# Layer A's masked score products as 32x32 diagonal blocks in one kept PSUM tile, and the norms' column sums from 32 stationary columns at a time

## The chip, the cores and the metric

The kernel runs on one core of one Trainium2 chip. The metric is the device time of one execution in microseconds (us): the median of 3 runs. The profile is of one further execution, taken with the hardware profiler, and its span is the time from its first to its last instruction. TensorE is called PE in the profile, VectorE DVE, ScalarE ACT, GpSimd POOL, and SyncE, which issues the DMAs, SP.

## What is computed

One inference step of a two-layer decoder trunk for 1024 prompt tokens and 8 single-token samples, all in fp32. Layer A is a gated linear recurrence (HGRN2) with 8 heads of 128 key and 256 value channels, layer B a spatial gating unit. Each layer starts with an RMS norm over the 1024 channels, and each is followed by a gated per-layer input with a norm of its own; a fifth norm ends the trunk. Cut to what matters here:

```python
def rmsnorm(x, g):
    return x * rsqrt(mean(x * x, axis=-1) + EPS) * g

def step(S, inp):                         # per chunk; b = cumsum of the log forget gates
    o_inter = einsum('bthk,bhkv->bthv', qb * exp(b), S)
    diff = where(causal, b[:, :, None] - b[:, None, :], -inf)
    att = einsum('bthk,bshk,btshk->btsh', qb, kb, exp(diff))
    o = o_inter + einsum('btsh,bshv->bthv', att, vb)
    S = exp(b_last) * S + einsum('bshk,bshv->bhkv', kb * exp(b_last - b), vb)
```

`att` is a masked score matrix whose decay between the two tokens depends on the channel. The kernel forms it for blocks of 128 tokens.

## The kernel before

**Tokens.** The 1032 tokens lie along the free axis, channels on the 128 partitions, in three chunks `c` of 384, 384 and 264 tokens (`W`); the first 256 of the last chunk are prompt tokens. `NT = (3, 3, 2)` counts the 128-token blocks of a chunk.

**Order of the work.** PE's instructions are issued in the order in which the program writes them (`manual_schedule`). The program writes the large projections (`proj`, L309, three fp32r products per 128x128 weight tile in `mm3`, L229 to L231) one after another, and between them runs small generator processes by a counter, `Ticks`: a projection of one chunk counts one tick at its half and, with its caller, one at its end, and a process that yields `n` goes on `n` ticks later. The instructions of the other engines are ordered by a planner by their place in the program and a priority (`tc.high_priority`). SP issues the DMAs in its queue's order.

**Layer A.** For each head `h` the projections f, q, the values (two halves) and the gate z (two halves) run over the three chunks. Beside them each chunk has a process `decay` (L661), which makes the score matrix in three parts, by the distance of the two tokens in a block of 128:

- Tokens of one group of 8: `X` and `Y` are q and k with decay factors about the middle of their group of 8 (L678 to L681). Four ticks later PE forms `Y^T X` for each block of 128 tokens into the PSUM tile `p0` (L685, one fp32 matmul of 128 stationary and 128 moving columns per block), and DVE copies the entries that `mask[:, 0]` names, 8x8 blocks on and above the diagonal, into the SBUF tile `am` (L696).
- Tokens of one group of 16 but of different groups of 8: DVE scales q and k in place, level by level (L722, L723, levels 1, 2, 4, ...). At level 8 PE forms `k^T q` in the same way into `p8` (L701), and DVE copies what `mask[:, 1]` names (L709).
- Larger distances: at levels 16, 32 and 64 PE forms only the rectangles that are wanted, 16x16, 32x32 and 64x64, into the tile `pC` (L719), which is kept for all of layer A and zeroed once (L563). DVE adds `am` and `pC` (L728).

`p0` and `p8` are both taken from one PSUM buffer (tag `pA`, one buffer), so each waits until DVE has read the one before. An fp32 matmul shows as two records in the trace, an fp32r matmul as one.

Other small PE work of layer A that the text names: transposes of the values (`pt_v`, L645), of k (`pt_k`, L738) and of the output (`pt_o`, L765), the state and output products (`pd`, `po`), and the samples' product `pos` (L856), in which eight fp32 matmuls of 32 stationary and 256 moving columns go in turn to PSUM partitions 0, 32, 64 and 96.

From head 1 on, the program order at chunk `c` is such that `pC` of one chunk (L719) is followed at once by `Y^T X` of the next chunk (L685).

**The norms.** `norm_sum` (L266) forms the sum of squares of each token over the partitions: for each block of 128 tokens and each part of the squares a matmul with the 128x128 squares stationary and one column of ones moving, into one column of the PSUM tile `pss` (L279). The first norm has four parts, the other four norms one (two in the last chunk). Then DVE adds epsilon (`rms_e`, L282), POOL takes the power -1/2 (`rsq`, L238), PE spreads the result over the partitions (`pbc`, L290) and DVE scales the rows (L303). Five norms of three chunks make 15 calls. In the first norm the calls stand between the per-layer input products (`ps_pple`) and the first projections.

## Time and profile before

| | before |
|---|---|
| median of 3 runs (lowest to highest) | 1895.23 us (1894.97 to 1897.35) |
| span of the profiled execution | 1892.0 us |
| mean granted TensorE clock | 0.994 |
| instructions of PE, DVE, ACT, POOL | 13130, 2977, 1859, 409 |
| records of the products L685 and L701 | 128 and 128 |
| records of the norms' sums L279 | 168 |

The profiled execution ran 1892.0 us from its first to its last instruction; the median of the runs is 3.2 us above that. A timeline row gives the start in us, the duration, the engine, the line and what is written and read, with `x6` for six records merged into one row. PE's matmuls overlap in it: the duration of one is its way through the array, and what it costs the next is the interval between their starts. `128*32 128x256` means 128 rows by 32 stationary columns, and an output of 256 columns. A row of the windows gives a stretch, its length, then for each engine that worked the busy time and the number of instructions in it, then the granted clock, the DMA share and GB/s.

### The profile page before, as it was taken

How to read it: one execution, taken by the hardware profiler on the slowest of the kernel's cores; microseconds unless marked ns; L12 is line 12 of the kernel's file. 1: busy time of each engine (PE TensorE's matmuls, PEld its weight loads, DVE VectorE, ACT ScalarE, POOL GpSimd, SP SyncE). 2: the span in 40 equal slices, each digit the busy share in tenths (PEclk: the TensorE clock that was granted, in tenths of full speed). 3: DMA queues.
4: the chain of work that ended last, by engine and by line, in shares of the span. 5: the costliest groups of instructions: out<-in, count | busy, mean ns of one | idle time of the engine just before them, and what ended most of it. 6: DMA issues, size and time to landing. Idle time of an engine off the chain costs nothing.

```text
span 1892.0 us, 34411 instructions
## 1 busy us (share of the span) xinstructions
PE 1861.4 (98%) x13130; PEld 1831.9 (97%) x13130; DVE 1331.5 (70%) x2977; ACT 866.1 (46%) x1859; POOL 396.2 (21%) x409
## 2 busy tenths in 40 slices
PE   9999999999999999999999999999999999999997
PEld 8999999999999999999999999999999999999997
DVE  5967677767767687678665845577777878777644
ACT  6463545444544546435344544433344335444342
POOL 4110001010000100000133333345544442000222
PEclk8999999999999999999999999999999999999998
DMA  6232323332222345854233343323334546953223
GB/s 216 75 108 78 109 73 111 126 130 97 94 79 93 101 139 158 287 194 135 94 127 119 115 143 92 95 79 116 111 116 148 184 134 205 302 184 106 63 90 113
DMA packets 155478, 243.15 MB, mean 129 GB/s; under 512 B 15088, under 2 KB 130480, under 8 KB 154288
## 3 DMA queue, kind: packets, MB, share of 16 engines
q1 hardware_dynamic: 155312, 240.94, 39.2%
q8 instruction: 103, 1.69, 0.4%
q14 instruction: 63, 0.52, 0.1%
HBM read 175.49 MB, written 65.40 MB: 127 GB/s over the span
## 4 chain that ended last, share of the span: by engine, by line
PE 81%; DVE 10%; DMA 5%; ACT 2%; issue 2%; POOL 1%; SPq 0%; DVEq 0%; ACTq 0%; POOLq 0%
PE ps_proj L229 19%; PE ps_proj L231 19%; PE ps_proj L230 19%; PE ps_o L229 2%; PE ps_o L230 2%; PE ps_o L231 2%; PE ps_d L229 2%; PE ps_d L231 2%; PE ps_d L230 2%; PE pC L719 1%; PE psp L1457 1%; DVE wlo L152 1%; PE pt_o L765 1%; PE p L685 1%; PE pt_v L645 1%
## 5 line engine op out<-in xcount | busy, mean ns | idle before, releaser
L229 PE MATMUL ps_proj<-bh,whi 128*128 128x384 f32 (+1 forms) x2392 | 764.9, 320 | 2.3 <-ACT pple_t L348 1.6
L231 PE MATMUL ps_proj<-bh,wlo 128*128 128x384 f32 (+1 forms) x2392 | 749.3, 313 | 1.5 <-DVE wlo L152 1.4
L230 PE MATMUL ps_proj<-bl,whi 128*128 128x384 f32 (+1 forms) x2392 | 748.0, 313 | 1.5 <-POOL bl L225 1.5
L229 PEld LDWEIGHTS ps_proj<-bh,whi 128*128 128x128 f32 x2392 | 451.0, 189 | 4.4 <-ACT pple_t L348 1.7
L230 PEld LDWEIGHTS ps_proj<-bl,whi 128*128 128x128 f32 x2392 | 451.4, 189 | 2.5 <-POOL bl L225 2.5
L231 PEld LDWEIGHTS ps_proj<-bh,wlo 128*128 128x128 f32 x2392 | 449.9, 188 | 2.7 <-DVE wlo L152 2.7
L152 DVE TENSOR_TENSOR wlo<-wstg,whi 128x1024 fp32r<-128x1024 f32 x148 | 184.6, 1248 | 97.7 <-ACT whi L151 96.3
L151 ACT CAST whi<-wstg 128x1024 fp32r<-128x1024 f32 x148 | 155.0, 1047 | 145.0 <-PE ps_proj L230 127.8
L151 ACT CAST shi<-ssum 128x512 fp32r<-128x512 f32 x128 | 79.1, 621 | 153.1 <-PE ps_proj L230 81.3
L152 DVE TENSOR_TENSOR slo<-ssum,shi 128x512 fp32r<-128x512 f32 x128 | 96.6, 757 | 8.5 <-ACT shi L151 8.0
L238 POOL TENSOR_TENSOR rsq<-rms_e,mhalf 128x3 f32<-128x3 f32 x15 | 14.1, 940 | 368.3 <-DVE rms_e L282 368.3
L229 PE MATMUL ps_proj<-xmh,shi 128*128 128x384 f32 x244 | 83.0, 340 | 1.1 <-DVE u L978 1.1
L231 PE MATMUL ps_proj<-xmh,slo 128*128 128x384 f32 x244 | 81.7, 335 | 0.0
L230 PE MATMUL ps_proj<-xml,shi 128*128 128x384 f32 x244 | 81.6, 335 | 0.0
L225 POOL TENSOR_TENSOR ql<-q,qh 128x384 fp32r<-128x384 f32 (+1 forms) x24 | 22.3, 929 | 254.0 <-ACT qh L224 254.0
L722 DVE TENSOR_TENSOR q<-q,t 128x192 f32<-128x192 f32 (+1 forms) x144 | 47.5, 331 | 39.1 <-PE pC L719 32.7
L229 PE MATMUL ps_o<-bh,whi 128*128 128x384 f32 (+1 forms) x232 | 73.2, 315 | 0.0
L230 PE MATMUL ps_o<-bl,whi 128*128 128x384 f32 (+1 forms) x232 | 72.7, 313 | 0.0
L231 PE MATMUL ps_o<-bh,wlo 128*128 128x384 f32 (+1 forms) x232 | 72.7, 313 | 0.0
L1466 POOL TENSOR_TENSOR s<-s,u 128x384 f32<-128x384 f32 (+1 forms) x48 | 54.7, 1140 | 68.5 <-DVE s L1460 67.9
L1205 DVE TENSOR_TENSOR tmp<-tmp,pj 128x384 f32<-128x384 f32 (+1 forms) x48 | 25.4, 530 | 56.4 <-ACT tmp L1204 50.4
L238 POOL TENSOR_TENSOR rsq<-ss_e,mhalf 128x3 f32<-128x3 f32 (+2 forms) x32 | 24.1, 752 | 192.9 <-DVE ss_e L759 192.9
(347 smaller groups left out, 3966.8 us busy)
## 6 DMA issues: line engine op xcount, KB each, us to landing
wstg<-in_wina SPq DMA_DIRECT2D x48, 512.0 KB, 3.7
wstg<-in_winb SPq DMA_DIRECT2D x48, 512.0 KB, 3.5
pj<-ppd SPq DMA_DIRECT2D x16, 516.0 KB, 5.0
S<-in_st SPq DMA_DIRECT2D x16, 512.0 KB, 4.6
vb<-vd SPq DMA_DIRECT2D x16, 512.0 KB, 4.8
out_so_s<-S SPq DMA_DIRECT2D x16, 512.0 KB, 3.5
wstg<-in_wouta SPq DMA_DIRECT2D x16, 512.0 KB, 3.5
wstg<-in_wgate SPq DMA_DIRECT2D x16, 512.0 KB, 3.7
```

Of the source, the lines that this page charges most:

```text
L151: A.copy(hi, src)
L152: V.tensor_tensor(lo, src, hi.bitcast(F32), ALU.subtract)
L225: last["lo"] = eng.tensor_tensor(lo, src, hi.bitcast(F32), ALU.subtract)
L229: PE.matmul(ps, wh, xh, start=first, stop=False, skip_group_check=more)
L230: PE.matmul(ps, wh, xl, start=False, stop=False, skip_group_check=more)
L231: PE.matmul(ps, wl, xh, start=False, stop=last, skip_group_check=more)
L238: G.tensor_tensor(y, e, mhalf[:, :n], ALU.pow)
L645: PE.transpose(pt[:, i, :], vf[:, i * P:(i + 1) * P], ident)
L685: PE.matmul(blk(p0, i), blk(Y, i), blk(X, i), start=True, stop=True)
L722: V.tensor_tensor(ql[:, :, 1, :], ql[:, :, 1, :], t2[:, :, 0:1].broadcast_to([P, n, lv]), ALU.mult)
L1205: V.tensor_tensor(gt[:, :w], gt[:, :w], pj[:, OFF[c]:OFF[c] + w], ALU.mult)
L1466: G.tensor_tensor(s[:, :w], s[:, :w], us[mm, c][:, :w], ALU.mult)
```

## The change

The two products are formed as 32x32 blocks on the diagonal alone, into one PSUM tile `pD` that is kept through layer A and zeroed once like `pC`; it takes the place of `p0` and `p8` in the tag `pA`. What lies outside the 32x32 blocks stays zero and is never copied, since both masks name entries within groups of 16. A product of a 128-token block is four matmuls of 32 stationary and 32 moving columns, each with all 128 rows, whose outputs lie at PSUM partitions 0, 32, 64 and 96. In `norm_sum` each matmul is likewise cut into four with 32 stationary columns, with outputs at the same four partition offsets.

```diff
@@ norm_sum
             for j, t in enumerate(parts):
-                PE.matmul(pss[:, i:i + 1], t[:, o:o + P], ones[:, 0:1],
-                          start=j == 0, stop=j == len(parts) - 1)
+                for b in range(0, P, 32):
+                    PE.matmul(pss[b:b + 32, i:i + 1], t[:, o + b:o + b + 32], ones[:, 0:1],
+                              start=j == 0, stop=j == len(parts) - 1)
@@ before layer A
     V.memset(pC, 0.0)
+    pD = pp.tile([P, 384], F32, name="pD", tag="pA", bufs=1)
+    V.memset(pD, 0.0)
@@ new
+    def diag(c, kt, qt):
+        for o in range(0, NT[c] * P, 32):
+            b = o % P
+            PE.matmul(pD[b:b + 32, o:o + 32], kt[:, o:o + 32], qt[:, o:o + 32], start=True, stop=True)
@@ decay
         yield 4
-        p0 = pp.tile([P, 384], F32, name="p0", tag="pA", bufs=1)
-        for i in range(NT[c]):
-            PE.matmul(blk(p0, i), blk(Y, i), blk(X, i), start=True, stop=True)
+        diag(c, Y, X)
...
-                V.copy_predicated(am[:, :w], mask[:, 0, :w], p0[:, :w])
+                V.copy_predicated(am[:, :w], mask[:, 0, :w], pD[:, :w])
...
-                p8 = pp.tile([P, 384], F32, name="p8", tag="pA", bufs=1)
-                for i in range(NT[c]):
-                    PE.matmul(blk(p8, i), blk(k, i), blk(q, i), start=True, stop=True)
+                diag(c, k, q)
...
-                V.copy_predicated(am[:, :w], mask[:, 1, :w], p8[:, :w])
+                V.copy_predicated(am[:, :w], mask[:, 1, :w], pD[:, :w])
```

## The prediction

> **What bounds the kernel now.** I read the page first, then the waits of the two engines that share layer A, then the timeline around each step that changes. The page's first part and its chain:

> ```profile
> PE 1861.4 (98%) x13130; PEld 1831.9 (97%) x13130; DVE 1331.5 (70%) x2977; ACT 866.1 (46%) x1859; POOL 396.2 (21%) x409
> ...
> PE 81%; DVE 10%; DMA 5%; ACT 2%; issue 2%; POOL 1%; SPq 0%; DVEq 0%; ACTq 0%; POOLq 0%
> ```

> The busy share of PE alone would prove little, since matmul ends are modelled; the chain says the same, that what ended last was 81% PE work. The waits between 60 and 760 us, where layer A runs (us in total, times, longest):

> ```profile
> PE pt_o L765 <- DVE oz L814: 5.0, 8, 1.6
> PE pt_v L645 <- DVE vl L225: 0.5, 1, 0.5
> PE pt_v L645 <- ACT vf L595: 0.2, 1, 0.2
> ...
> DVE Am L696 <- PE p L685: 23.9, 8, 4.4
> ```

> The first three lines are all of PE's waits there, 5.7 us in 700. None is for operands of the products (L685, L701). DVE, the next busiest engine, waits for PE and not the other way round. So an interval taken from PE in layer A should shorten the layer, and prices are to be read as intervals between matmul starts, not as durations.

> **Today's price of the two products.** Each is issued per 128-token block as one fp32 matmul with 128 stationary columns, which the trace records as two records:

> The timeline (start, duration, engine, line, records merged into the row) shows such a burst, and further on the sample product L856, which is needed below:

> ```profile
> 81.52 0.34 PE L231 MATMUL ps_proj<-bh,wlo 128*128 128x384 f32 x1
> 81.70 0.83 PE L685 MATMUL p<-X,Y 128*128 128x128 f32 x6
> 82.28 0.37 PE L229 MATMUL ps_proj<-bh,whi 128*128 128x264 f32 x1
> 82.49 0.28 PE L230 MATMUL ps_proj<-bl,whi 128*128 128x264 f32 x1
> ...
> 118.79 0.28 PE L230 MATMUL ps_proj<-bl,whi 128*128 128x264 f32 x1
> 118.91 0.28 PE L231 MATMUL ps_proj<-bh,wlo 128*128 128x264 f32 x1
> 119.13 1.07 PE L856 MATMUL pos<-S,qm 128*32 128x256 f32 x16
> 120.13 0.44 PE L229 MATMUL ps_proj<-bh,whi 128*128 128x384 f32 x1
> 120.41 0.34 PE L230 MATMUL ps_proj<-bl,whi 128*128 128x384 f32 x1
> 120.58 0.34 PE L231 MATMUL ps_proj<-bh,wlo 128*128 128x384 f32 x1
> ```

> ```profile
> L685 PE MATMUL p<-X,Y 128*128 128x128 f32 x128 | 19.6, 286 | 0.0
> ```

> From 81.52 to 82.49 are 0.97 us. Two ordinary intervals would be 0.17 (120.41 to 120.58, 384 columns) and 0.12 (118.79 to 118.91, 264 columns), so six records cost 0.68 us, 0.113 each, with nothing extra for going in or out. The group's row counts 128 records for L685, and by the code L701 has as many: 24 bursts each, 16 of six (chunks 0 and 1) and 8 of four (chunk 2).

> **The new price.** After the change the same bursts have four times as many records of 32 stationary by 32 moving columns, rotating over PSUM partitions 0, 32, 64, 96. The trace of before has this form already: L856 (32 stationary and 256 moving columns, the same rotation) and part of pC. Going into L856, 118.91 to 119.13 is 0.22 against 0.12: 0.10 us extra. Coming out, the second interval, 120.13 to 120.41, is 0.28 against 0.17: 0.105 extra. How many records had begun by a given moment is in the windows (the count behind PE busy), first L856, then pC:

> ```profile
> 119.05:119.16 0.11, 0.03 (x4) 0.04 (x5) 0.00 (x0) 1.00 0.00 0
> 119.05:119.36 0.31, 0.23 (x4) 0.16 (x8) 0.00 (x0) 1.00 0.00 0
> 119.05:119.40 0.35, 0.27 (x8) 0.19 (x12) 0.00 (x0) 1.00 0.00 0
> 119.05:119.84 0.79, 0.71 (x16) 0.42 (x16) 0.00 (x0) 1.00 0.00 0
> ...
> 97.60:97.83 0.23, 0.17 (x25) 0.17 (x26) 0.00 (x0) 1.00 1.11 387
> 97.60:98.01 0.41, 0.35 (x36) 0.35 (x36) 0.00 (x0) 1.00 1.11 377
> ```

> Four records start within 0.03 us, then none for 0.2 us, then the next four: four blocks in four column groups stream side by side, and a batch takes about 0.215 us for 256 moving columns (16 records in four batches, 1.00 us from 119.13 to 120.13, of which 0.025 is the first weights and 0.1 the drain at the end). In pC 25 records of (nearly all) 16 columns start in 0.17 us, under 7 ns each; the next 11, of 32 columns in only two groups, take 0.18, so 15 to 16 ns each, that is 0.03 us for one record in every group. With four groups I therefore take 0.03 us for a batch of four records, 7.5 ns each. The bounds are 6.5 (the spacing in pC and of four starts in L856) and 15 ns (no gain from four groups over two).

> A burst of B batches then costs: 0.10 in, 0.025 first weights, 0.03(B-1) for the starts, 0.02 inside the last batch, 0.125 from its last start to the next matmul (0.03 stream, 0.1 drain), 0.105 after: 0.345 + 0.03B. Six batches: 0.525 against 0.68, four: 0.465 against 0.45. A lone burst of chunk 0 or 1 gains 0.155, one of chunk 2 loses 0.015. The neighbours matter:

> ```profile
> 167.95 1.02 PE L719 MATMUL pC<-q,k 128*16 128x16 f32 x42
> 168.91 0.94 PE L685 MATMUL p<-X,Y 128*128 128x128 f32 x6
> 169.68 0.49 PE L645 MATMUL pt_v<-ident,vf 128*128 128x128 f32 x3
> 169.92 0.42 PE L229 MATMUL ps_proj<-bh,whi 128*128 128x384 f32 x1
> ...
> 84.86 0.55 PE L645 MATMUL pt_v<-ident,vf 128*128 128x128 f32 x3
> 85.17 0.37 PE L229 MATMUL ps_proj<-bh,whi 128*128 128x264 f32 x1
> ```

> - Transposes behind a burst take 0.24 us after full-width products (169.68 to 169.92) and 0.31 after pC (84.86 to 85.17): coming out costs them 0.07, not 0.105, so a burst of six there saves 0.68 - 0.10 - 0.32 - 0.07 = 0.19. These are L685 of chunk 0 (8) and L701 of chunk 0 and, from head 1, chunk 1 (15): 23 x 0.19 = 4.4.
> - From head 1 on, L685 of chunks 1 and 2 stands right behind pC of the chunk before, which pays for coming out today (168.91 to 169.68 is 0.77). There six records go from 0.77 to 0.32 + 0.07: 0.38 saved, 7 times, 2.7; four go from 0.54 to 0.26 + 0.105: 0.18, 7 times, 1.3.
> - Two lone bursts of head 0: 0.3. Nine of chunk 2: 0.1 lost.

> Layer A: 4.4 + 2.7 + 1.3 + 0.3 - 0.1 = 8.6 us. What DVE does with the products (L696, L709) keeps its size. pD's wait for DVE's last read is the wait that the tag's one buffer had; it was not among PE's waits. The added memset of pD on DVE is like pC's, 0.38 us:

> ```profile
> L563 DVE MEMSET pC<- x1: 378/378/378, 55.0 to 55.0; 128x384 f32 x1
> ```

> DVE's waiting for PE hides it; uncovered, 0.4. Layer-A ticks are counted in projections, so no wait of PE gets nearer by more than a fraction of a us.

> **The norms.** Their stationary side is the 128-column load, their moving side one column:

> ```profile
> L279 PE MATMUL pss<-ones,ssq 128*128 128x1 f32 x72 | 9.8, 237 | 0.0
> L279 PE MATMUL pss<-ones,sq 128*128 128x1 f32 x72 | 8.2, 246 | 0.0
> L279 PE MATMUL pss<-ones,sql 128*128 128x1 f32 x24 | 4.4, 251 | 1.4 <-ACT sql L258 1.4
> ...
> 14.33 2.73 PE L279 MATMUL pss<-ones,sq 128*128 128x1 f32 x24
> 16.92 0.42 PE L229 MATMUL ps_pple<-ph,whi 128*128 128x384 f32 x1
> ```

> 24 records take 2.59 us, 0.108 each, near the 0.113 above, which I use (2.7 for 24). The 168 records are three bursts of 24 (first norm), eight of 6 and four of 12 (the other four norms; two parts in the last chunk). By the same formula: six, 0.68 to 0.525, eight times 0.155 = 1.2; twelve, 1.36 to 0.705, three times 0.655 = 2.0. The fourth burst of twelve is in the tail, where only ACT's last squares are waited for:

> ```profile
> 1879.53 0.38 PE L279 MATMUL pss<-ones,sql 128*128 128x1 f32 x2 [1.40 <-ACT sql L258]
> ```

> Behind that wait stand ten records, 1.1 us, and become forty, about 0.35: 0.7 off the end of the program, since everything after it waits for this sum. For the first norm 24 batches give 1.065; no row shows 96 such records in a row, so I take 1.2 and save 1.5 per burst, 4.5 in all, if the start follows PE. At the second burst it does:

> ```profile
> 27.01 0.16 DVE L282 TENSOR_SCALAR rms_e<-pss 128x3 f32<-128x3 f32 x1 [1.75 <-PE pss L279]
> ...
> 27.74 0.51 ACT L224 CAST bh<-tmp 128x384 fp32r<-128x384 f32 x1 [1.92 <-DVE tmp L303]
> ...
> 28.59 0.69 PE L229 MATMUL ps_proj<-bh,whi 128*128 128x384 f32 x1 [1.61 <-ACT pple_t L348]
> ...
> 17.62:21.10 3.48, 3.48 (x14) 3.48 (x13) 0.00 (x0) 1.77 (x4) 2.54 (x3) 0.51 1.04 343
> ```

> DVE stands in its queue at rms_e until the burst is over, ACT behind DVE, and PE behind ACT. The last row (clock, third number from the end) says that the clock was halved right after the first long burst; a shorter burst may avert that, worth up to 1.7 us, which I leave to the range. So is the other end: another load or POOL's sums hold the start, and only one burst's 1.5 counts.

> **Sum.** 8.6 + 1.2 + 2.0 + 0.7 + 4.5 = 17.0 us off the profiled 1892.0, so a span of 1875.0; the median of the runs lies 3.2 above the span, which gives 1895.2 - 17.0 = 1878.2.

> [...] In L856 four records start within 0.03 us, in pC 25 within 0.17. [...]

> **Rivals.**
> - *Records in a long burst are bound by issue (slower).* The change adds 768 records to the products and 504 to the norms, 1696 in all now, so each ns per record is 1.7 us. At 7.5 ns 17.0 are saved, so break-even lies at 7.5 + 17.0/1.7 = 17.5 ns. If queued records run out and each then costs 22.5 ns, three times as much, 15 x 1.7 = 25.5 us are lost: 8.5 slower, 1903.7. For it: 96 records in a row were never seen. Against it: pC starts 36 in 0.35 us. Chance 0.06. [...]
> - *Two groups at a time, not four*: 15 ns per record, 7.5 x 1.7 = 12.7 less saved, 1890.9. Against it: L856's batches of four. Chance 0.08.
> - *PE's gain turns into waits* (a planner order that moves because PE has more instructions, DVE or the weights' loads late): about 1893 to 1895. For it: pt_o already waits for DVE. Against it: DVE waits more for PE than PE for DVE. Chance 0.06.

> **Numbers.** Main case 0.80, 1878.2. Its own ends: 6.5 ns per record (1.7 less) and the clock kept (1.7 and some of the start's chain) down to 1873; one burst alone of the start (+3.0), 10 ns per record (+4.2), up to 1885, to 1887 with some planner loss. So 1873 to 1887, which leaves out the rivals. A measurement of this kernel tells 0.2% (3.8 us) from nothing: faster (under 1891.4) 0.80 + 0.08, same 0.06, slower 0.06.

> **What would show it.** The products at 24 records in about 0.2 us from first start to last, lone bursts about 0.16 shorter between the surrounding projections, those behind pC 0.4; heads 1 to 6 each about 1.1 us shorter (0.38 + 0.18 + three times 0.19); long norm bursts of 1.0 to 1.3 us; the first projection (28.59) 1.5 to 4 us earlier; no new wait of PE on DVE. Wrong if records start 15 ns or more apart, if coming out costs more than 0.23 us, or if PE's idle time grows by what its bursts lose.

## The result and the profile after

The changed kernel takes 1878.1 us (median of 4 runs, 1875.5 to 1879.8), the kernel before beside it 1895.1 (1894.1 to 1897.4): a ratio of 0.9912, with an interval of 0.9898 to 0.9926. A second set of runs gave 1876.1 (ratio 0.9899, 0.9883 to 0.9915). The profiled spans are 1892.0 before and 1878.0 after. Lines move by one to four: L279 is now L280, L685 and L701 are both L663, pC's L719 is L723, the transposes' L645 is L648.

The page's first part and its chain, of after:

```profile
PE 1844.7 (98%) x14402; PEld 1802.6 (96%) x14402; DVE 1332.6 (71%) x2978; ACT 866.0 (46%) x1859; POOL 400.9 (21%) x409
...
PE 83%; DVE 8%; DMA 4%; ACT 2%; issue 1%; POOL 1%; SPq 0%; DVEq 0%; ACTq 0%; POOLq 0%
```

PE has 1272 records more and is busy 16.7 us less; the chain is still PE's. The groups of PE's shapes show the new records, four times as many with 32 stationary columns:

```profile
L663 PE MATMUL pD<-X,Y 128*32 128x32 f32 x512 | 9.0, 200 | 0.0
...
L280 PE MATMUL pss<-ones,ssq 128*32 128x1 f32 x288 | 5.1, 174 | 0.0
```

PE's busy time on the first product fell from 19.6 us (128 records) to 9.0 (512). The timeline of after, at the places that the prediction used:

```profile
14.65 0.98 PE L280 MATMUL pss<-ones,sq 128*32 128x1 f32 x96
15.56 0.44 PE L229 MATMUL ps_pple<-ph,whi 128*128 128x384 f32 x1
...
22.38 0.44 PE L229 MATMUL ps_proj<-bh,whi 128*128 128x384 f32 x1
...
74.75 0.34 PE L231 MATMUL ps_proj<-bh,wlo 128*128 128x384 f32 x1
75.02 0.40 PE L663 MATMUL pD<-X,Y 128*32 128x32 f32 x24
75.35 0.39 PE L229 MATMUL ps_proj<-bh,whi 128*128 128x264 f32 x1
75.57 0.29 PE L230 MATMUL ps_proj<-bl,whi 128*128 128x264 f32 x1
...
160.76 1.02 PE L723 MATMUL pC<-q,k 128*16 128x16 f32 x42
161.72 0.40 PE L663 MATMUL pD<-X,Y 128*32 128x32 f32 x24
162.04 0.55 PE L648 MATMUL pt_v<-ident,vf 128*128 128x128 f32 x3
162.35 0.42 PE L229 MATMUL ps_proj<-bh,whi 128*128 128x384 f32 x1
...
248.91 1.02 PE L723 MATMUL pC<-q,k 128*16 128x16 f32 x42
```

- The lone burst: 74.75 to 75.57 is 0.82 us, against 0.97 before. Going in costs 0.27 (0.17 without), coming out 0.33 to the next matmul and then 0.22 instead of 0.12.
- Behind pC: 160.76 to 162.35 is 1.59, against 1.97 before (167.95 to 169.92): 0.38 less.
- From one head's pC to the next, 160.76 to 248.91, are 88.15 us; before, the row `257.22 ... pC` follows the one at 167.95 after 89.27. So a head is 1.12 us shorter.
- The first norm's burst lies 0.91 before the next matmul, against 2.59, and 96 records of it start in 0.82 us:

```profile
14.64:14.85 0.21, 0.20 (x23) 0.20 (x27) 1.00 1.05 380
14.64:15.05 0.41, 0.40 (x47) 0.40 (x50) 1.00 1.09 378
14.64:15.25 0.61, 0.59 (x72) 0.60 (x74) 1.00 1.04 355
14.64:15.48 0.84, 0.82 (x96) 0.83 (x96) 1.00 1.06 357
```

These are the windows of after for that line alone: the count behind PE busy grows by 24 or 25 in each 0.2 us, 8.2 to 8.5 ns each from the first to the last. A column group is here the set of 32 stationary columns whose results go to one of the PSUM partition offsets 0, 32, 64 and 96.

PE's waits over the whole span of after:

```profile
PE pt_o L769 <- DVE oz L818: 4.4, 9, 0.8
PE ps_d L229 <- DVE c L1001: 3.7, 2, 3.1
```

The second is new in size: before, the same wait came to 1.3 us in all and 0.7 at the longest. It is taken up below.

### The profile page after: what moved, and what is told of

Its sections match the earlier page's. It is cut to its first block, busy times and chain, and to the rows that moved or that the text cites. A ratio compares the mean times of both kernels' runs of the same rounds, so it can differ in the third digit from the quotient of the medians.

```text
span 1878.0 us, 36932 instructions
## 1 busy us (share of the span) xinstructions
PE 1844.7 (98%) x14402; PEld 1802.6 (96%) x14402; DVE 1332.6 (71%) x2978; ACT 866.0 (46%) x1859; POOL 400.9 (21%) x409
## 4 chain that ended last, share of the span: by engine, by line
PE 83%; DVE 8%; DMA 4%; ACT 2%; issue 1%; POOL 1%; SPq 0%; DVEq 0%; ACTq 0%; POOLq 0%
PE ps_proj L229 20%; PE ps_proj L231 20%; PE ps_proj L230 20%; PE ps_d L229 2%; PE ps_o L229 2%; PE ps_d L231 2%; PE ps_o L230 2%; PE ps_d L230 2%; PE ps_o L231 2%; PE pC L723 1%; PE pt_v L648 1%; DMA vn<-vraw 1%; PE pt_o L769 1%; DVE wlo L152 1%; PE psp L1461 1%
## 5 line engine op out<-in xcount | busy, mean ns | idle before, releaser
L229 PE MATMUL ps_proj<-bh,whi 128*128 128x384 f32 (+1 forms) x2392 | 764.8, 320 | 1.1 <-ACT u L978 1.1
L230 PE MATMUL ps_proj<-bl,whi 128*128 128x384 f32 (+1 forms) x2392 | 748.6, 313 | 2.7 <-DVE bl L225 1.4
L231 PE MATMUL ps_proj<-bh,wlo 128*128 128x384 f32 (+1 forms) x2392 | 748.8, 313 | 1.6 <-DVE wlo L152 1.4
L230 PEld LDWEIGHTS ps_proj<-bl,whi 128*128 128x128 f32 x2392 | 451.4, 189 | 4.9 <-DVE bl L225 3.4
L229 PEld LDWEIGHTS ps_proj<-bh,whi 128*128 128x128 f32 x2392 | 450.9, 188 | 3.1 <-ACT u L978 1.6
L231 PEld LDWEIGHTS ps_proj<-bh,wlo 128*128 128x128 f32 x2392 | 450.1, 188 | 2.5 <-DVE wlo L152 2.5
L229 PE MATMUL ps_proj<-xmh,shi 128*128 128x384 f32 x244 | 83.1, 340 | 1.0 <-DVE u L982 1.0
L230 PE MATMUL ps_proj<-xml,shi 128*128 128x384 f32 x244 | 81.8, 335 | 0.3 <-DVE xml L225 0.3
L231 PE MATMUL ps_proj<-xmh,slo 128*128 128x384 f32 x244 | 81.7, 335 | 0.0
L225 POOL TENSOR_TENSOR ql<-q,qh 128x384 fp32r<-128x384 f32 (+1 forms) x24 | 22.2, 926 | 253.4 <-ACT qh L224 253.4
L229 PE MATMUL ps_o<-bh,whi 128*128 128x384 f32 (+1 forms) x232 | 73.2, 316 | 0.0
L231 PE MATMUL ps_o<-bh,wlo 128*128 128x384 f32 (+1 forms) x232 | 72.7, 313 | 0.0
L230 PE MATMUL ps_o<-bl,whi 128*128 128x384 f32 (+1 forms) x232 | 72.7, 313 | 0.0
```

The lines of the kernel that those rows point to most:

```text
L225: last["lo"] = eng.tensor_tensor(lo, src, hi.bitcast(F32), ALU.subtract)
L229: PE.matmul(ps, wh, xh, start=first, stop=False, skip_group_check=more)
L230: PE.matmul(ps, wh, xl, start=False, stop=False, skip_group_check=more)
L231: PE.matmul(ps, wl, xh, start=False, stop=last, skip_group_check=more)
```

## The experiments

Theory: PE sets the pace; four records in four column groups take 8 ns each; a change of the stationary width costs about 0.1 us going in and 0.2 coming out; the gain is the sum of the bursts. Rivals: the gain of the start comes from the clock and not from the records; the order of the groups does not matter; in long bursts the instructions do not come fast enough ("issue").

### Products alone, norms alone, first norm alone

Three versions split the change: `diag` and `pD` with the old `norm_sum`; the new `norm_sum` with the old products; and the new form for the first norm only:

```diff
+                step = 32 if isinstance(ssq, list) else P
-                for b in range(0, P, 32):
+                for b in range(0, P, step):
```

> The products as 32x32 blocks, the norms' sums as before. Theory (PE bounds layer A, records of four column groups run side by side at 7.5 to 8.5 ns): bursts of 24 records take 0.20 us from first start to last, heads 1 to 6 take 1.1 us less each, the start of the program is as before (first f projection at 28.6 us plus or minus 0.5), and the total is 8.6 to 9.2 us under before, about 1886. Rival (the gain comes from the shorter start and its clock, and what layer A saves on PE is given back as waits): under 4 us saved, 1891 or more.

> The norms' sums from 32 columns at a time, the products as before. Theory: the start gains 5 to 6 us by the end of the first norm (three bursts 1.5 each, and one stretch at half clock less), the eight short bursts 0.17 each, three of 12 records 0.63 each, the tail 0.7: 9 to 10 us in all, about 1885.5. Rival (the first norm's gain is lost in DVE's and POOL's own order): 5 us at most, 1890 or more.

> Only the first norm, the one with four parts, in blocks of 32 columns; all else as before. Theory: 5 to 6 us saved, all of it by 65 us after the start, about 1889.5; of it 4.5 are the three bursts themselves, the rest the first halving of the clock that does not come. Rival: the bursts alone, 4.5 with the clock halved as before, or 1.5 where other loads hold the start.

Measured against 1894.6 before (10 runs): products alone 1883.4 (ratio 0.9941, 0.9927 to 0.9955), 11.2 us less; norms alone 1883.8 (0.9945, 0.9933 to 0.9958), 10.8 less; the first norm alone 1888.1 (0.9967, 0.9956 to 0.9979), 6.5 less. The spans are 1882.8, 1885.3 and 1885.9. All three agree with the theory within their intervals. The two halves add up to 22.0 us, against 17.0 and 19.0 for the whole in its two sets of runs, so neither half needs the other; why the sum is 3 to 5 us larger was not followed up. With the products alone the gain is larger than expected (8.6 to 9.2), but not all of it is the products': in the profile of that version PE wins 9.0 us against before from 46 to 705 us, and 2.4 more at the end of layer A, up to 765 us.

### The blocks of one column group in a row

```diff
-        for o in range(0, NT[c] * P, 32):
+        for o in sorted(range(0, NT[c] * P, 32), key=lambda o: o % P):
```

> As the changed kernel, but diag issues its blocks sorted by PSUM partition, so that all blocks of one column group follow each other. Theory (a column group takes one record at a time, about 30 ns, and only different groups overlap): bursts of 24 take 0.65 to 0.75 us from first start to last in place of 0.20, 1024 records times 22 ns or 20 to 23 us more than the changed kernel, about 1900 and slower than before. Rival (small records are fast in any order, for what costs is the width of the load): bursts stay at 0.20 us and the time at 1878.

Measured: 1882.4 (ratio 0.9933, 0.9919 to 0.9947), 4.3 us over the first set of runs of the changed kernel, not 20. Timeline and windows of this version at the lone burst:

```profile
75.27 0.65 PE L663 MATMUL pD<-X,Y 128*32 128x32 f32 x24
75.84 0.39 PE L229 MATMUL ps_proj<-bh,whi 128*128 128x264 f32 x1
```

```profile
75.25:75.30 0.05, 0.03 (x1) 0.03 (x2) 1.00 0.00 0
75.25:75.40 0.15, 0.13 (x5) 0.13 (x7) 1.00 0.00 0
75.25:75.50 0.25, 0.23 (x11) 0.23 (x13) 1.00 0.00 0
75.25:75.60 0.35, 0.33 (x19) 0.33 (x21) 1.00 0.00 0
```

The burst lies 0.57 before the next matmul instead of 0.33. At first one record starts every 26 to 32 ns, as I had priced a group by itself; but then 6 and 8 start in each 0.1 us, as they can if records of the next group start beside those that still stand in line for the first. The order matters, but less than the theory without such overlap said. The total understates it: from 46 to 705 us this version loses 8.3 to 8.5 us against the two profiles of the changed kernel, about two fifths of the 20 to 23 expected, and wins part of that back behind layer A, where its execution had no wait of PE at 810 us. That the order does not matter is wrong too.

### Every block twice

```diff
-        for o in range(0, NT[c] * P, 32):
+        for o in 2 * list(range(0, NT[c] * P, 32)):
```

> As the changed kernel, but diag issues its list of blocks twice in a row (the same values are written again): 1024 more records, no more changes between full-width and 32-column work. Theory: 7.9 ns per record, bursts of 48 in 0.39 us, 8 us more than the changed kernel. Rival (issue at 22 ns or more once the queue is empty): 20 us or more. If the theory holds, a burst's remaining price of 0.34 us is that of going in and out.

Measured: 1889.1 (7 runs, ratio 0.9962, 0.9948 to 0.9976), 13.0 over the changed kernel in the same set (1876.1). The timeline of this version:

```profile
75.85 0.63 PE L663 MATMUL pD<-X,Y 128*32 128x32 f32 x48
76.41 0.39 PE L229 MATMUL ps_proj<-bh,whi 128*128 128x264 f32 x1
```

24 records more take 0.23 us (0.56 against 0.33 before the next matmul), 9.7 ns each, and 16 more in the short bursts 0.126, 7.9 ns. 32 x 0.23 + 16 x 0.126 are 9.4 us, near the 8.1 expected. The other 3.6 are not in the bursts. The traces place them: against the second profile of the changed kernel (below) this one loses 9.0 us from 46 to 705 us, then 3.3 at the end of layer A, where PE waits 1.7 us more and the clock is at half from 748.6 to 752.0 us, and 2.3 from there to 820 us, at a wait for DVE of 2.8 us, behind which the clock is at half once more. At both places two executions of one kernel differ too, so these losses are not put down to the second pass.

### The changed kernel once more

> The changed kernel once more, to see what of its first profile returns. Theory: the bursts and the shortened start return in every execution; the wait of 3.1 us of PE for DVE near 810 us, with the clock halved behind it, hangs on when a DMA lands and need not. Median 1875 to 1880; a profile without that wait has a span of 1872 to 1875. Rival: the wait is made by the change and comes back.

Measured: 1876.1, with a profiled span of 1873.6, 4.4 shorter than that of the first profile. What differs is mostly one place. The timelines of after, of this run and of before there (DVE, or PE with its wait in brackets):

```profile
805.72 0.56 DVE L425 TENSOR_TENSOR raw<-raw 128x384 f32<-128x384 f32 x1 [3.95 <-DMA raw<-ozd]
...
810.88 0.69 PE L229 MATMUL ps_d<-bh,whi 128*128 128x384 f32 x1 [3.06 <-DVE c L1001]
```

```profile
809.98 0.44 PE L229 MATMUL ps_d<-bh,whi 128*128 128x384 f32 x1 [2.13 <-DVE c L1001]
```

```profile
818.83 0.56 DVE L424 TENSOR_TENSOR raw<-raw 128x384 f32<-128x384 f32 x1 [2.54 <-DMA raw<-ozd]
```

DVE waits for a load of `ozd`, and what it then makes is what PE waits for. From before to after DVE's step came 13.1 us earlier (818.83 to 805.72), while PE's own work had come 15.6 us earlier by then; the difference became PE's wait. Behind the longer wait the clock was at half (windows of after, the third number from the end):

```profile
809.90:813.30 3.40, 2.42 (x8) 2.42 (x9) 3.40 (x7) 0.62 (x1) 0.00 (x0) 0.50 0.67 223
```

In the second profile it was not. So the half clock did not return, but the wait did, at 2.13 us: the median lies where I expected it, but the rival, that the change makes the wait, is not settled. Against it, the wait does not go with the gain: it was 0.6 us in both profiles of before, 1.9 with the norms alone, 0.7 with the products alone, absent with the blocks sorted by group, and 2.8 with every block twice. Why the load lands later in some executions was not tried.

### pC's rectangles at 32 columns as well

```diff
-                        PE.matmul(pC[b:b + l, o + l:o + 2 * l], kb, qb, start=True, stop=True)
+                        for i in range(0, l, 32):
+                            u = min(l, 32)
+                            PE.matmul(pC[b + i:b + i + u, o + l:o + 2 * l], kb[:, i:i + u], qb, start=True, stop=True)
```

> As the changed kernel, but pC's 64x64 rectangles are formed as two of 32 stationary and 64 moving columns, so that pC and the blocks that follow it stay in one width. Theory (each change of width costs PE a drain and an uncovered load): pC bursts of 42 records become 48 and take 0.15 us less from first to last start, 24 times, and the 14 bursts behind pC start about 0.14 us sooner: 5 to 6 us less than the changed kernel, about 1873. Rival (only going to and from full width costs, 32 to 64 is free): 0 to 1 us.

Measured: 1871.1 (ratio 0.9878, 0.9858 to 0.9899), 5.0 less than the changed kernel in the same set. The timeline of this version, same head as above:

```profile
161.98 0.80 PE L725 MATMUL pC<-q,k 128*16 128x16 f32 x46
...
162.63 0.40 PE L663 MATMUL pD<-X,Y 128*32 128x32 f32 x22
162.96 0.55 PE L648 MATMUL pt_v<-ident,vf 128*128 128x128 f32 x3
163.26 0.42 PE L229 MATMUL ps_proj<-bh,whi 128*128 128x384 f32 x1
```

161.98 to 163.26 is 1.28 against 1.59. Of these 0.31 us, 0.17 are gone between pC's first and last start, and 0.14 at the border, where the records of pC and pD now mix: the first of pD starts at 162.58, the last of pC, which the program writes before it, at 162.62. At the border a change of width, from 64 to 32, has been taken away. Inside pC it was one too, from 32 to 64: of after's 42 records, 36 have started by 161.11 (windows of pC in after, the count behind PE busy), and none starts in the next 0.11 us.

```profile
160.70:161.11 0.41, 0.35 (x36) 0.35 (x36) 0.00 (x0) 1.00 0.00 0
160.70:161.22 0.52, 0.46 (x36) 0.42 (x36) 0.00 (x0) 1.00 0.00 0
```

Behind that change the records of 64 columns start 0.058 apart, and in this version two records of 32 take nearly as long, about 0.056; four groups in place of two gained little here. From 46 to 705 us this version wins 5.8 to 6.0 us against the two profiles of the changed kernel, as expected.

The same with the memset of `pD` issued behind the first weights' split instead of at the head of DVE's queue (`with tc.issue_after(last["lo"].ins):`):

> As the run before it, and the zeroing of pD is queued on DVE behind the first norm's last split, in place of near the top of DVE's queue. Theory: the first matmul of the program starts 0.3 us earlier, and the rest follows: 0.3 us, less than the timing can tell. Rival: nothing, since the start waits for DMAs anyway.

Measured: 1871.1 (ratio 0.9871, 0.9855 to 0.9887). Of the DVE rows of after, the memset stands ahead of the cast that PE's first matmul needs:

```profile
1.58 0.38 DVE L566 MEMSET pD<- 128x384 f32 x1
1.87 0.41 DVE L117 CAST zr<-zf 128x512 fp32r<-128x512 f32 x1
```

Before, the cast began at 1.53, and with the late memset it does so again; PE's first matmul moves from 2.33 back to 2.02. The end does not move: by 8 us the two versions stand level to 0.1, since what PE needs next waits for other things. These two versions are the fastest of all, 24 us under the kernel before.

### The first norm thrice and twice, and the kernel before again

The records of the first norm's sums are issued three times, and twice (the later pass overwrites the earlier):

```diff
+            for _ in range(3 if isinstance(ssq, list) else 1):
```

> The first norm's three bursts are issued three times over (288 records of 32 stationary columns and one moving column instead of 96; the first two passes are overwritten by the last, so the result is the same). Both theories price the records alike: two passes more of 96 at 8.5 ns are 1.6 us per burst, so a burst of 2.45 us from first to last start, nearly the 2.59 of the burst in the kernel before; three bursts make 4.9 us, about 1881 to 1883 against 1876 to 1878 of the changed kernel. They differ on the clock. Theory (the length of the stretch with only one-column products brings the halving, whatever the width of the stationary side): the granted clock falls to 0.5 at the next step of 3.4 us behind the first burst, between about 17 and 22 us, as it did in the kernel before and in the version with the old norms, and this costs up to 1.7 us more for each halving. Rival (the 128 stationary columns of the records bring it, or their weight loads): the clock stays at 1.00 from 14 to 22 us, as in the changed kernel.

> The kernel before, once more, for its clock alone: if the long burst of one-column products brings the halving, the granted clock is at 0.5 again right behind the first burst (17.7 to 21.1 us, as in the first profile). If it was a matter of the single execution, it may stay at 1.00 there.

> The first norm's three bursts issued twice (192 records each; the first pass is overwritten). With 288 records PE ran 175 and 228 records at 8 to 9 ns and then stood 4.75 and 2.6 us with nothing that the profile shows, and in each gap one packet of 16 KB of the instruction queue landed. From before to changed, 1272 records more brought 10 packets more, so a packet holds about 128 records, 1.05 us of them. Theory (PE runs through its fetched code faster than the queue brings more): two of three bursts or fewer stand, where the code in hand ends inside the burst; a burst without a stand costs 0.82 us more than in the changed kernel, one with a stand 2.6 to 4.8 more on top; about 1879 without a stand, 1881 to 1888 with them. Rival (any stretch over some 100 records stands, as a queue of fixed length would have it): all three bursts stand at one and the same count of records, above 96 and below 175. That they stand at the same count of 175 or more would also be told from this run: then none of the theory's dependence on where the packet ends is left.

Thrice: 1891.0 (8 runs, ratio 0.9974, 0.9962 to 0.9985), 8 over the upper end of the expected time; twice: 1886.5 (one run). The timeline of the version with three, then of that with two:

```profile
15.39 1.63 PE L281 MATMUL pss<-ones,sq 128*32 128x1 f32 x175
...
21.77 1.71 PE L281 MATMUL pss<-ones,sq 128*32 128x1 f32 x113 [4.75 <-issue]
```

```profile
14.43 1.63 PE L281 MATMUL pss<-ones,sq 128*32 128x1 f32 x175
20.76 0.43 PE L281 MATMUL pss<-ones,sq 128*32 128x1 f32 x17 [4.71 <-issue]
29.44 1.78 PE L281 MATMUL pss<-ones,sq 128*32 128x1 f32 x192
```

The first burst stops after 175 records and stands 4.7 us for nothing that the profile shows; the second burst of the version with two, of the same 192 records, does not stand at all. So it is no queue of a fixed length. The DMA queues in the stretch 16.0 to 20.7 us of the version with two:

```profile
q1 hardware_dynamic: 1293, 1.77, 106.0%
q8 instruction: 1, 0.02, 1.5%
```

One packet of the instruction queue landed there, while the DMA engines were full. Over the whole kernel this queue has the following packets and MB, before and after (in the next experiment there are 169):

```profile
q8 instruction: 103, 1.69, 0.4%
```

```profile
q8 instruction: 113, 1.85, 0.4%
```

1272 records more brought 10 packets, so a packet of 16 KB holds about 128 records. Counted in the order of PE's matmuls, the stands come at number 223 in both versions, and in that with three also at 606, 862 and 990: 383, 256 and 128 apart, always whole packets. By these counts PE had run out of its code.

As a test of the clock the version with three decides nothing, since PE stood before the clock fell. The kernel before, once more (span 1890.7), kept its clock behind the first long burst, the second of the two outcomes that I had named (its windows); it was at half later, from 25.5 to 32.4 us:

```profile
17.70:21.10 3.40, 3.40 (x27) 3.40 (x26) 0.61 (x2) 3.05 (x6) 2.90 (x4) 1.00 1.09 370
```

### The diagonal blocks eight times

```diff
-        for o in range(0, NT[c] * P, 32):
+        for o in 8 * list(range(0, NT[c] * P, 32)):
```

> Each product's diagonal blocks issued eight times over, in layer A: bursts of 192 and 128 records of the same form instead of 24 and 16, where the DMA engines are busy 0 to 0.4 of the time and not all of it as at the start. Records alone: 7 times the 0.234 and 0.126 us that the second pass cost, 32 and 16 bursts: 66 us, about 1940 to 1945. Theory (PE outruns the instruction queue; a packet takes its time to land, less where the DMA engines are free): bursts of 192 stand in part of the cases, by 1 to 2.6 us each, none by 4 us; with 10 to 30 stands 10 to 60 us on top, 1955 to 2000. Rival (the stands come from the full DMA engines at the start alone): no stand of over 0.3 us in layer A, 1940 to 1945.

Measured: 2007.1 (one run). PE's waits from 60 to 800 us, and one burst of the timeline:

```profile
PE pD L663 <- issue: 31.6, 19, 2.7
...
PE pt_v L648 <- issue: 2.8, 1, 2.8
```

```profile
174.92 1.58 PE L663 MATMUL pD<-q,k 128*32 128x32 f32 x163
178.57 0.45 PE L663 MATMUL pD<-q,k 128*32 128x32 f32 x29 [2.07 <-issue]
```

The windows row of this stand (the DMA share is the last number but one):

```profile
176.50:178.57 2.07, 0.00 (x1) 0.00 (x0) 1.42 (x2) 0.00 (x0) 0.00 (x0) 1.00 0.00 0
```

The stands are there with idle DMA engines too, 2.07 us in this row, and the longest of all, 2.8 us, at a share of 0.69; at the start it was 4.7 with the engines full. They come in part of the bursts: as the theory of the code's packets has it, and not a matter of the start. Between stands the records keep 8.6 to 9 ns through 192 in a row. Counted as above, the stands lie at 989, 1500, 2394, 2649, 2904, 3160 and so on, again whole packets of 127.7 records apart. From the end of one packet to the moment that PE goes on with the one after the next are 1.7 to 4.5 us here and 5.9 at the first stand of the start, by my estimate the time that a packet takes; how many packets PE holds and what starts the next one, no trace shows. The time is 7 us over the upper end that I gave; the mean granted clock of this run was 0.988, and 0.995 in the changed kernel, which is one part of it.

## Why the prediction was right, and where not

The shifts below are of the same matmul between two profiles, counted over the trace.

| step | predicted | before to after | before to the second profile of after |
|---|---|---|---|
| start, up to 46.8 us | 4.5 | 5.8 | 6.0 |
| products of layer A, to 705 us | 8.6 | 8.7 | 8.5 |
| end of layer A, to 758 us | none | 1.7 | 1.0 |
| wait for DVE at 810 us, clock, to 827 us | none | -5.7 | -1.5 |
| short norms, and what lies between | 3.2 | 3.4 | 4.1 |
| tail | 0.7 | 0.1 | 0.3 |
| sum | 17.0 | 14.0 | 18.4 |

**The price of a record and of going in and out was right.** Lone bursts gain 0.15 (predicted 0.155), bursts behind pC 0.38 to 0.39 and 0.19 (0.38 and 0.18), those before transposes 0.19 to 0.20 (0.19), a head 1.12 (1.13); lone bursts of chunk 2 lose 0.013 (0.015). The window rows of L856 and pC, forms that stood in the kernel already, gave all of it. That the first median met the forecast to 0.1 us is luck all the same: the second set of runs lies 2.1 under it, and the two profiled spans fell by 14.0 and 18.4 us, with gains and losses in them that the forecast did not have.

**The norms** gain 0.17 per burst of six (0.155), 0.63 per burst of twelve (0.655), 1.57 per first-norm burst (1.5): the 1.2 us taken for 96 records was a little high.

**The start** came out near the forecast, but what the clock did in it is not settled. The first projection starts at 22.38 instead of 28.59, 6.2 earlier; I had given 1.5 to 4. But in the second profile of before it starts at 26.81, with the same wait of 1.61: 1.8 of the 6.2 belong to a halving of the clock that one execution of before had and another had not. Against that one the changed kernel gains 3.8 by 46 us, not 5.8. I had said that a shorter burst may avert the halving: none of nine profiles with the short form as the change has it shows it right behind the first burst, and two of three with the long form do. That is a hint and no proof. Elsewhere the clock was at half during or behind stretches in which PE stood: for 3.4 us (24.9 to 28.2 in after), 6.8 (809.9 to 816.7 there) or 10.2 (18.1 to 28.3 in the version with three passes of the first norm). Executions of one kernel differ in it, as the two of before do from 17.7 to 21.1 us (0.50 and 1.00); what decides when the clock halves, no trace shows.

**The memset of pD was not hidden**, as I had it, "by DVE's waiting": it stands ahead of the cast that PE's first matmul waits for, and that matmul came 0.3 later. The version with the late memset shows that this cost the end nothing.

**"No new wait of PE on DVE" was wrong.** Layer A has none, but behind it PE stood 3.06 us at 810 in one execution and 2.13 in another, for a chain of DMA and DVE that had come forward by less than PE. My "no new wait" had looked at layer A alone and put the stages behind it at nothing. It looks like the third rival in small, a gain that runs into the next stage's load, and 1.5 to 5.7 us were lost there. But with pC at 32 columns PE comes to this place 18.3 us earlier than before and waits 0.7, and with every block twice only 2.4 earlier and waits 2.8, so it is not shown that the gain makes the wait; what decides when the load lands stays open.

**The tail** gained 0.74 at its last pbc, and the end only a part of it:

```profile
1865.75 0.24 PE L280 MATMUL pss<-ones,sql 128*32 128x1 f32 x8 [1.39 <-ACT sql L258]
...
1867.54 1.03 PE L291 MATMUL pbc<-ident,rsq 128*128 128x128 f32 x6 [1.28 <-POOL rsq L238]
```

From the wait's end to pbc are 1.79 us; before, pbc came at 1882.06, 2.53 behind 1879.53. What follows, DVE's rows and the stores, is not PE's: from the last pbc to the end took 8.9 and 8.6 us in the two profiles of before and 9.8 and 9.7 in those of after. Why is open.

**The first rival** (long bursts run out of issue) is a true mechanism that the changed kernel just misses. I had put its point of decision in ns per record; it lies in the records per stretch of time. The two packet ends that lie closest together in after are 6.7 us apart, the first at 15.0 us, inside the 96 records of the first norm; at the start a packet took 5.9 us, by the estimate above. At 8.6 ns per record PE goes through the 128 records of a packet in 1.1 us, and in the versions with longer bursts it stood 0.4 to 4.8 us.

## What to carry to other kernels

Price a new shape by the starts of a like shape that the trace already holds, and add what it costs to change the stationary width, going in and coming out (here about 0.1 us in and 0.2 out): small products paid for it once per visit, so put all that have one width side by side. Count how many records stand in a row: here PE stood in part of the bursts of 128 to 288 records, where it used up packets of code (128 records each) faster than one in 1.7 to 5.9 us by estimate, and the profile showed that only as a wait for "issue". And when a stage becomes shorter, look at the first load that the next one needs, since that load may not come earlier by as much (here the step behind it came 13.1 us earlier, PE's own work 15.6).
